# Row sums of a softmax: partial sums on GpSimd, ones-products once per pair of heads, and another step order

## The chip, the cores and the metric

The kernel runs on one core of a Trainium2 chip. The metric is the device time of one execution in microseconds (us); for a kernel that was timed in several runs it is their median. Engines are named as in the profile: PE (TensorE), ACT (ScalarE), DVE (VectorE), POOL (GpSimd), SP (the engine that issues most DMAs).

## What is computed

A two-layer backbone over 512 latent tokens of width 1024, in float32. Layer 0 mixes tokens by an 8-head latent attention and a Fourier mixer; layer 1 by a convolution module and a short gated convolution; each layer ends with a SwiGLU. All modulations come from a matrix-vector product with the conditioning vector (below: the ada jobs). The change lies in the attention of layer 0, which for each head is

```python
kt = jnp.concatenate([k_ctx, k], axis=1)      # 256 context + 512 latent keys
s = jnp.einsum('bqhd,bhkd->bhqk', q, kt) * scale
p = jax.nn.softmax(s, axis=-1)
o = jnp.einsum('bhqk,bhkd->bqhd', p, vt)
...
mix = o @ a_w_out                              # after concatenation with the Fourier part
```

with 512 queries, 768 keys, 96 elements of q and k and 64 of v per head.

## The kernel before, in words

Matmul operands are split into a high and a low part (`split`, L94: ACT casts the high part at L95, DVE, or in layer 1 partly GpSimd, subtracts at L96), and `mm3` (L115 to L117) takes three products. Weights arrive as units of 128x1024 floats (`unit`, L102): SP issues the load (L105) into one of three buffers of the tag `wraw`, and the halves go to `whi` and `wlo`, five buffers each.

Attention goes head by head, with keys in the partitions: the score tile is transposed, so that exp(score - maximum) can be taken by ACT straight out of PSUM. For head h the steps are

- `m0`, `m1` (`a_max`): the maxima of the **next** head. PE computes rough scores (L821, L822), DVE reduces them from PSUM (L824, L825); `m1` ends with the maximum of two small SBUF tiles (L827) and its negation into `nmx` (L828).
- `row` (`a_row`): PE transposes `nmx` (L836) and ACT copies the row to row 96 of the next head's `qT` (L837), so that a score matmul subtracts the maximum itself. The next head's first score (L850) needs it.
- `s0`, `s1`, `s2` (`a_score`): each two tiles of 128 keys by 512 queries, three matmuls each (L850 to L852) and an exponential on ACT (L853) into a 128x1024 tile: a buffer of `wraw` (named `praw`) or a fixed slot.
- `tq`, `tk`, `tc` (`a_trq`, `a_trk`): transposes of q and k of the head after the next, taken out of PSUM by ACT (L787) and DVE (L788).
- After two heads (a pair): `v0` to `v2`, or `p0` to `p2` when they come among the next pair's steps (`a_av`): the products with v (L865), and behind them four products with a matrix of ones (L870), which sum the exponentials over the keys. In the last of them ACT copies the sums (L874) and the output (L876) to SBUF.
- `n0` to `n2` (`a_nrm`): the sums are picked out by a small matmul with `sel` (L884) and inverted by DVE (L886); PE spreads the inverse over 64 rows (L892); DVE multiplies (L898), and the result is split into `o_t`, which out_proj reads.

`EVEN_ORDER` and `ODD_ORDER` give the order in which a head's steps are written, and `weave` puts the ada jobs between them, each of which is one load and one DVE operation of 128x1024 with two SBUF inputs (L153). The last pair's products and normalization stand in `END_ORDER`, between the first steps "O" of out_proj: L525 to L552, `unit` m, then the products of output block m. A scheduler then moves the instructions on each engine by its own estimates, so the written order is not the order of an engine. Each engine takes its own instructions strictly in order. PSUM has eight buffers (`ps`, L82).

Of the kernel before, what the change touches and what calls it, by code (L numbers as in the profile page):

```python
# [9 lines left out]
F32 = mybir.dt.float32  # L10
# [7 lines left out]
P = 128  # L18
D = 1024
KT = 8  # L20
S = 512
# [3 lines left out]
NH = 8  # L25
# [8 lines left out]
FH = (5, 14)  # L34
PH = (2, 3)
HU, NF, NK2 = (14, 13, 8), 5, 5
EVEN_ORDER = "m0 p1 p2 s0 m1 s1 s2 n0 tk row n1 n2 tq tc"
ODD_ORDER = "s0 s1 m0 s2 m1 v0 row tk tc tq"
END_ORDER = "p1 p2 O n0 O n1 n2 O O O"
OA = 4  # L40
MIX_ORDER = "G0 G3 G2 C0 G1 C2 C3 C1"
SA0, SA1, SC, PU, RB, TB, AB = 1, 20, 15, 6, 3, 5, 2
# [3 lines left out]
UB = 5  # L46
# [14 lines left out]
def tile_dit(  # L61
# [16 lines left out]
    def nm(base):  # L78
        uid[0] += 1
        return f"{base}_{uid[0]}"  # L80

    def ps(shape=(P, S)):  # L82
        return pp.tile([P, S], F32, tag="ps", name=nm("ps"))

    def t2k(n=S):
        return tmp.tile([P, n], F32, tag="t", bufs=TB, name=nm("t"))
# [753 lines left out]
    def a_score(h, tp):  # L840
        def f():
            kT, qT = kTt[h % 2], ost["qT"][:, h % 2]
            raw = ost["pb"][(3 * h + tp) % 6]
            if raw is None:
                raw = units.tile([P, D], F32, tag="wraw", bufs=RB, name=nm("praw"))
            for s in range(2):
                t = tp * 2 + s
                c = slice(t * P, (t + 1) * P)
                p = ps()
                T.matmul(p, kT[:97, 0, c], qT[:97, 0, :], start=True, stop=False)  # L850
                T.matmul(p, kT[:96, 0, c], qT[:96, 1, :], start=False, stop=False)  # L851
                T.matmul(p, kT[:96, 1, c], qT[:96, 0, :], start=False, stop=True)  # L852
                A.activation(raw[:, s * S:(s + 1) * S], p, AF.Exp, scale=float(DH) ** -0.5)  # L853
            ost["p", h, tp] = raw
        return f

    def a_av(j, tp):
        def f():
            if tp == 0:
                ost["o", j], ost["su", j] = ps(), ps()  # L860
            p, su = ost["o", j], ost["su", j]
            for s in range(2):
                t = tp * 2 + s
                for x in range(2):
                    T.matmul(p[64 * x:64 * x + 64, :], vh[t][:, 2 * j + x, :], ost["p", 2 * j + x, tp][:, s * S:(s + 1) * S],  # L865
                             start=(t == 0), stop=(t == 5))
            for s in range(2):
                for x in range(2):
                    g = 32 * (2 * x + s)
                    T.matmul(su[g:g + 32, :], ones[:, 0:32], ost["p", 2 * j + x, tp][:, s * S:(s + 1) * S],  # L870
                             start=(tp == 0), stop=(tp == 2), tile_position=(0, g))
            if tp == 2:
                ost["sr", j] = t2k()
                A.copy(ost["sr", j], su)  # L874
                ost["or"] = t2k()
                A.copy(ost["or"], p)  # L876
        return f

    def a_nrm(j, i):
        def f():  # L880
            if i == 0:
                st = ps()
                for t in range(4):
                    T.matmul(st[:, 2 * t:2 * t + 2], ost["sr", j][:, t * P:(t + 1) * P], sel, start=True, stop=True)  # L884
                r = sm.tile([P, 8], F32, tag="rs", name=nm("rs"))
                V.reciprocal(r, st[:, 0:8])  # L886
                ost["r"] = r
            elif i == 1:
                ost["rb"] = ps()
                for t in range(4):  # L890
                    for x in range(2):
                        T.matmul(ost["rb"][64 * x:64 * x + 64, t * P:(t + 1) * P],  # L892
                                 ost["r"][:, 2 * t + x:2 * t + x + 1].to_broadcast([P, 64]), ident, start=True, stop=True)
            else:
                if j % 2 == 0:
                    o_t.append(slot((9, 10)[j // 2], [P, 2, 2, S], F32R))
                d = o_t[j // 2][:, j % 2]
                V.tensor_mul(ost["or"], ost["or"], ost["rb"])  # L898
                split(d[:, 0, :], d[:, 1, :], ost["or"])
        return f  # L900
# [7 lines left out]
    for h in range(NH):  # L908
        made = {f"s{i}": a_score(h, i) for i in range(3)}
        if h + 1 < NH:  # L910
            made.update(m0=a_max(h + 1, 0), m1=a_max(h + 1, 1), row=a_row(h + 1))
        if h + 2 < NH:
            made.update(tq=a_trq(h + 2), tk=a_trk(h + 2, 2, 4), tc=a_trk(h + 2, 0, 2))
        j = h // 2
        made.update({f"v{i}": a_av(j, i) for i in range(3)})
        if j > 0:
            made.update({f"p{i}": a_av(j - 1, i) for i in range(3)})
            made.update({f"n{i}": a_nrm(j - 1, i) for i in range(3)})
        asteps += [made[x] for x in (EVEN_ORDER, ODD_ORDER)[h % 2].split() if x in made]
    g1s = ada_jobs(0, "g1", 16, 8)  # L920
    s2s = ada_jobs(0, "s2", 24, 16)
# [20 lines left out]

    oout = out_proj(w_out0, 8, mix(0), mix(1), mods[0, "g1"], "n2_0", n2_0)
    end = {f"p{i}": a_av(NH // 2 - 1, i) for i in range(3)}
    end.update({f"n{i}": a_nrm(NH // 2 - 1, i) for i in range(3)})
    last, pos = [], 0
    for x in END_ORDER.split():
        if x == "O":
# [485 lines left out]
```

## Time and profile before

| | |
|---|---|
| median of 3 runs | 1205.73 us (1203.50 to 1205.98) |
| the profiled execution | 1207.13 us, its span 1205.4 us |
| granted TensorE clock of the span | 0.995 of full speed |
| attention, first score to first product of the last pair | 147.76 to 239.59 us of the span |
| out_proj's second unit begins | 254.93 us |

The profile shows one execution. Times in it are microseconds from the start of the span; matmul records overlap, since they are pipelined, so the distance from start to start tells what one costs. Products with 64 or 32 output columns of weights in float32 leave two records per matmul.

### The profile page before, as it was taken

The page shows a single profiled execution, that of the slowest core. Times are in us where ns is not written, and L with a number is a line of the kernel's source. Part 1 is how long each engine was busy: PE and PEld are TensorE (multiplying, and loading weights), DVE is VectorE, ACT ScalarE, POOL GpSimd, SP SyncE. Part 2 cuts the span into 40 slices and gives each one's busy share as a digit, 9 for nine tenths or more (in the row PEclk, how much of TensorE's full clock was granted, in tenths as well). Part 3 has the DMA queues.
Part 4 walks back from the last instruction along what each step waited for, and adds up shares of the span by engine and source line. Part 5 has one row for each costly group of instructions (what it writes and reads, how often), then busy time and mean ns, then how long its engine had stood idle before and what let it go on. Part 6 is the DMA issues. An engine that isn't in the chain of part 4 may idle for free.

```text
span 1205.4 us, 16811 instructions
## 1 busy us (share of the span) xinstructions
PE 1180.0 (98%) x6627; PEld 994.7 (83%) x6627; DVE 800.9 (66%) x1302; ACT 480.0 (40%) x787; POOL 128.0 (11%) x110
## 2 busy tenths in 40 slices
PE   8999999999999999999999899999899999999998
PEld 6777856569988888888888888889898899989987
DVE  7989877647655556554443799967867458746861
ACT  5545455535332323232222554335644235424530
POOL 1013300000000000000004495100000000000000
PEclk9999999999999999999999999999999999999999
DMA  9872033383265565555555232221357336634341
GB/s 345 299 290 86 1 110 101 112 271 124 86 210 191 195 207 184 186 182 166 166 166 154 74 105 89 86 88 36 134 149 207 115 98 171 188 96 128 92 140 53
DMA packets 52226, 177.25 MB, mean 147 GB/s; under 512 B 5681, under 2 KB 6577, under 8 KB 51890
## 3 DMA queue, kind: packets, MB, share of 16 engines
q1 hardware_dynamic: 49410, 166.21, 41.5%
q0 software_dynamic: 2736, 9.96, 4.9%
q8 instruction: 52, 0.85, 0.3%
q14 instruction: 28, 0.23, 0.1%
HBM read 174.05 MB, written 2.10 MB: 146 GB/s over the span
## 4 chain that ended last, share of the span: by engine, by line
PE 90%; DVE 4%; DMA 3%; ACT 2%; issue 1%; SPq 0%; POOL 0%; ACTq 0%; DVEq 0%
PE ps L115 21%; PE ps L117 21%; PE ps L116 21%; PE ps L1135 14%; PE ps L865 2%; DMA wraw<-in_w 1%; PE ps L707 1%; DVE wlo L96 1%; PE ps L580 1%; PE ps L850 1%; PE ps L851 1%; PE ps L852 1%; ACT whi L95 1%; PE ps L870 1%; DVE t L210 1%
## 5 line engine op out<-in xcount | busy, mean ns | idle before, releaser
L115 PE MATMUL ps<-s,whi 128*128 128x512 f32 (+1 forms) x1067 | 395.8, 371 | 7.0 <-ACT whi L95 5.8
L116 PE MATMUL ps<-s,whi 128*128 128x512 f32 (+1 forms) x1067 | 391.7, 367 | 2.1 <-DVE s L216 2.1
L117 PE MATMUL ps<-s,wlo 128*128 128x512 f32 (+1 forms) x1067 | 391.7, 367 | 1.4 <-DVE wlo L96 1.4
L95 ACT CAST whi<-wraw 128x1024 fp32r<-128x1024 f32 (+1 forms) x133 | 135.7, 1022 | 319.0 <-PE ps L116 184.4
L115 PEld LDWEIGHTS ps<-s,whi 128*128 128x128 f32 x1067 | 202.1, 190 | 42.4 <-ACT whi L95 7.1
L117 PEld LDWEIGHTS ps<-s,wlo 128*128 128x128 f32 x1067 | 202.0, 189 | 36.9 <-DVE wlo L96 3.2
L116 PEld LDWEIGHTS ps<-s,whi 128*128 128x128 f32 x1067 | 202.2, 190 | 35.7 <-DVE s L216 2.3
L96 DVE TENSOR_TENSOR wlo<-wraw,whi 128x1024 fp32r<-128x1024 f32 (+2 forms) x113 | 134.0, 1186 | 89.9 <-ACT whi L95 86.0
L1135 PE MATMUL ps<-s,whi 128*128 128x256 f32 x912 | 168.1, 285 | 2.1 <-DVE t L1155 2.1
L1135 PEld LDWEIGHTS ps<-s,whi 128*128 128x128 f32 x912 | 143.1, 192 | 4.5 <-DVE t L1155 3.5
L1135 PE MATMUL ps<-s,wlo 128*128 128x256 f32 x456 | 128.5, 283 | 0.0
L271 DVE SCALAR_TENSOR_TENSOR x<-ps,m_g,x 128x512 f32<-128x512 f32 (+1 forms) x67 | 43.9, 661 | 104.9 <-PE ps L117 104.9
L153 DVE CUSTOM_DVE_ANT_0 ada<-ada,scb,vec 128x1024 f32<-128x1024 f32 x80 | 100.1, 1278 | 1.1 <-DMA ada<-in_ada 1.1
L1135 PEld LDWEIGHTS ps<-s,wlo 128*128 128x128 f32 x456 | 87.4, 192 | 0.0
L1102 POOL DMA_DIRECT2D s<-in_w x19 | 16.8, 884 | 606.3 <-DMA s<-in_w 414.6
L96 DVE TENSOR_TENSOR wlo<-s,whi 128x1024 fp32r<-128x1024 f32 x57 | 69.4, 1221 | 11.7 <-ACT whi L95 11.3
L95 ACT CAST whi<-s 128x1024 fp32r<-128x1024 f32 x57 | 58.8, 1044 | 28.0 <-PE ps L116 19.1
L1007 DVE TENSOR_TENSOR t<-ps,t 128x512 f32<-128x512 f32 x22 | 15.2, 692 | 71.3 <-PE ps L117 71.3
L1247 DVE SCALAR_TENSOR_TENSOR ps<-s,vec,ps 128x512 f32<-128x512 f32 x78 | 55.8, 748 | 1.4 <-ACT ps L1244 0.9
L96 POOL TENSOR_TENSOR wlo<-wraw,whi 128x1024 fp32r<-128x1024 f32 x20 | 49.2, 2462 | 30.9 <-ACT whi L95 27.0
L116 PE MATMUL ps<-s,s 128*128 128x256 f32 (+1 forms) x160 | 50.2, 315 | 0.0
L117 PE MATMUL ps<-s,s 128*128 128x256 f32 (+1 forms) x160 | 50.1, 314 | 0.0
(274 smaller groups left out, 1608.2 us busy)
## 6 DMA issues: line engine op xcount, KB each, us to landing
ada<-in_ada SPq DMA_DIRECT2D x82, 512.0 KB, 4.4
wraw<-in_w SPq DMA_DIRECT2D x74, 512.0 KB, 3.7
s<-in_w SPq DMA_DIRECT2D x19, 768.0 KB, 5.1
wraw<-in_w_in SPq DMA_DIRECT2D x20, 512.0 KB, 3.3
s<-in_w SPq DMA_DIRECT2D x38, 256.0 KB, 4.3
s<-in_w POOLq DMA_DIRECT2D x19, 512.0 KB, 5.5
s<-in_ada SPq DMA_DIRECT2D x16, 512.0 KB, 6.7
wraw<-in_w_out SPq DMA_DIRECT2D x16, 512.0 KB, 3.8
```

Of the source, the lines that this page charges most:

```text
L95: A.copy(hi, src)
L96: (eng or V).tensor_sub(lo, src, f32(hi))
L115: T.matmul(o, wh, ah, start=start, stop=False)
L116: T.matmul(o, wh, al, start=False, stop=False)
L117: T.matmul(o, wl, ah, start=False, stop=stop)
L153: i = V.tensor_tensor_reduce(raw, raw, scv, 1.0, vc("ada_b", idx), ALU.mult, ALU.add, accum_out=dst)
L271: V.scalar_tensor_tensor(X[m][:, a:b], psum, gcol, X[m][:, a:b], ALU.mult, ALU.add)
L865: T.matmul(p[64 * x:64 * x + 64, :], vh[t][:, 2 * j + x, :], ost["p", 2 * j + x, tp][:, s * S:(s + 1) * S], start=(t == 0), stop=(t == 5))
L1007: V.tensor_mul(g, p, held.pop(f))
L1102: G.dma_start(s13, w[:, :D], accum_op=ALU.add)
L1135: T.matmul(o, w, b, start=start and kk == 0 and i == 0, stop=kk == 3 and i == 2, skip_group_check=True)
L1247: V.scalar_tensor_tensor(dst, cp[:, w:w + S], vec[:, o + w:o + w + 1], src, ALU.mult, ALU.add)
```

## The change

Per head, GpSimd adds the three tiles of exponentials elementwise into one tile `psum` of 128x1024, a buffer of the tag `wlo`: one addition after the exponentials of `s1`, one after those of `s2`. The ones-products read `psum` and are made once per pair, as a step of their own: it is the new `n0`, which also copies the sums, and the old `n0` to `n2` become `n1` to `n3`. The three orders are rewritten for it; in them `m0`, `m1` and `row` stand at other places too.

```diff
--- before.py
+++ after.py
@@ -34,9 +34,9 @@
 FH = (5, 14)
 PH = (2, 3)
 HU, NF, NK2 = (14, 13, 8), 5, 5
-EVEN_ORDER = "m0 p1 p2 s0 m1 s1 s2 n0 tk row n1 n2 tq tc"
-ODD_ORDER = "s0 s1 m0 s2 m1 v0 row tk tc tq"
-END_ORDER = "p1 p2 O n0 O n1 n2 O O O"
+EVEN_ORDER = "m0 p1 p2 n0 s0 m1 s1 n1 s2 tk n2 row n3 tq tc"
+ODD_ORDER = "s0 m0 s1 m1 s2 v0 tk row tc tq"
+END_ORDER = "p1 p2 O n0 n1 O n2 n3 O O O"
 OA = 4
 MIX_ORDER = "G0 G3 G2 C0 G1 C2 C3 C1"
 SA0, SA1, SC, PU, RB, TB, AB = 1, 20, 15, 6, 3, 5, 2
@@ -852,26 +852,24 @@
                 T.matmul(p, kT[:96, 1, c], qT[:96, 0, :], start=False, stop=True)
                 A.activation(raw[:, s * S:(s + 1) * S], p, AF.Exp, scale=float(DH) ** -0.5)
             ost["p", h, tp] = raw
+            if tp == 1:
+                ost["sum", h] = units.tile([P, D], F32, tag="wlo", bufs=UB, name=nm("psum"))
+                G.tensor_add(ost["sum", h], ost["p", h, 0], raw)
+            elif tp == 2:
+                G.tensor_add(ost["sum", h], ost["sum", h], raw)
         return f
 
     def a_av(j, tp):
         def f():
             if tp == 0:
-                ost["o", j], ost["su", j] = ps(), ps()
-            p, su = ost["o", j], ost["su", j]
+                ost["o", j] = ps()
+            p = ost["o", j]
             for s in range(2):
                 t = tp * 2 + s
                 for x in range(2):
                     T.matmul(p[64 * x:64 * x + 64, :], vh[t][:, 2 * j + x, :], ost["p", 2 * j + x, tp][:, s * S:(s + 1) * S],
                              start=(t == 0), stop=(t == 5))
-            for s in range(2):
-                for x in range(2):
-                    g = 32 * (2 * x + s)
-                    T.matmul(su[g:g + 32, :], ones[:, 0:32], ost["p", 2 * j + x, tp][:, s * S:(s + 1) * S],
-                             start=(tp == 0), stop=(tp == 2), tile_position=(0, g))
             if tp == 2:
-                ost["sr", j] = t2k()
-                A.copy(ost["sr", j], su)
                 ost["or"] = t2k()
                 A.copy(ost["or"], p)
         return f
@@ -879,13 +877,23 @@
     def a_nrm(j, i):
         def f():
             if i == 0:
+                su = ps()
+                for s in range(2):
+                    for x in range(2):
+                        g = 32 * (2 * x + s)
+                        T.matmul(su[g:g + 32, :], ones[:, 0:32], ost["sum", 2 * j + x][:, s * S:(s + 1) * S],
+                                 start=True, stop=True, tile_position=(0, g))
+                sr = t2k()
+                A.copy(sr, su)
+                ost["sr", j] = sr
+            elif i == 1:
                 st = ps()
                 for t in range(4):
                     T.matmul(st[:, 2 * t:2 * t + 2], ost["sr", j][:, t * P:(t + 1) * P], sel, start=True, stop=True)
                 r = sm.tile([P, 8], F32, tag="rs", name=nm("rs"))
                 V.reciprocal(r, st[:, 0:8])
                 ost["r"] = r
-            elif i == 1:
+            elif i == 2:
                 ost["rb"] = ps()
                 for t in range(4):
                     for x in range(2):
@@ -915,7 +923,7 @@
         made.update({f"v{i}": a_av(j, i) for i in range(3)})
         if j > 0:
             made.update({f"p{i}": a_av(j - 1, i) for i in range(3)})
-            made.update({f"n{i}": a_nrm(j - 1, i) for i in range(3)})
+            made.update({f"n{i}": a_nrm(j - 1, i) for i in range(4)})
         asteps += [made[x] for x in (EVEN_ORDER, ODD_ORDER)[h % 2].split() if x in made]
     g1s = ada_jobs(0, "g1", 16, 8)
     s2s = ada_jobs(0, "s2", 24, 16)
@@ -942,7 +950,7 @@
 
     oout = out_proj(w_out0, 8, mix(0), mix(1), mods[0, "g1"], "n2_0", n2_0)
     end = {f"p{i}": a_av(NH // 2 - 1, i) for i in range(3)}
-    end.update({f"n{i}": a_nrm(NH // 2 - 1, i) for i in range(3)})
+    end.update({f"n{i}": a_nrm(NH // 2 - 1, i) for i in range(4)})
     last, pos = [], 0
     for x in END_ORDER.split():
         if x == "O":
```

Line numbers behind the additions shift: the products with v are L870 in the changed kernel, the ones-products L884, the copies of outputs and of sums L874 and L887, the product with `sel` L892, the reciprocal L894, the spreading L900, the multiplication L906. The additions are L857 and L859.

How the instructions stand on POOL in the attention of layer 0, where there were none before (`praw`, `s_245` and `s6b` hold exponentials, heads 0 and 1 shown; 16 in all, two per head):

```order
L857 TENSOR_TENSOR psum_1454<-praw_1421,s_245_1297 128x1024
L859 TENSOR_TENSOR psum_1454<-psum_1454,praw_1456 128x1024
L857 TENSOR_TENSOR psum_1531<-s_245_1297,praw_1520 128x1024
L859 TENSOR_TENSOR psum_1531<-psum_1531,s6b_1298 128x1024
```

All sixteen read two tiles in SBUF.

DVE in head 2, where the maxima of head 3 are finished (`mx`; `s_242` is `nmx`, `rs` the inverse sums, `ada` an ada job). Before:

```order
L825 TENSOR_REDUCE mx_1591<-ps_1636 128x2
L827 TENSOR_TENSOR mx_1591<-mx_1591 128x4
L828 TENSOR_SCALAR s_242_1291<-mx_1591 128x4
L153 ISA ada_1669,m_g_935<-ada_1669,scb,vec 128x1024
L153 ISA m_g_935 128x1
L886 RECIPROCAL rs_1677<-ps_1672 128x8
```

Now:

```order
L825 TENSOR_REDUCE mx_1592<-ps_1634 128x2
L894 RECIPROCAL rs_1663<-ps_1658 128x8
L827 TENSOR_TENSOR mx_1592<-mx_1592 128x4
L153 ISA ada_1665,m_g_935<-ada_1665,scb,vec 128x1024
L153 ISA m_g_935 128x1
L828 TENSOR_SCALAR s_242_1291<-mx_1592 128x4
```

The reciprocal has come ahead of the maxima, and an ada job stands between the two small operations that finish them. The heads 3 and 6 have the ada job at the same place.

ACT at the end of attention (`t` is a copy of sums or outputs, `whi` a unit's high part). Before:

```order
L95 CAST whi_2222<-wraw_2221 128x1024
L874 COPY t_2217<-ps_2189 128x512
L876 COPY t_2219<-ps_2188 128x512
L95 CAST whi_2261<-wraw_2260 128x1024
L159 ACTIVATE m_s_936<-m_s_936,vec 128x1
L95 CAST whi_2304<-wraw_2303 128x1024
L95 CAST whi_2336<-wraw_2335 128x1024
```

Now:

```order
L95 CAST whi_2207<-wraw_2206 128x1024
L874 COPY t_2204<-ps_2188 128x512
L95 CAST whi_2253<-wraw_2252 128x1024
L159 ACTIVATE m_s_936<-m_s_936,vec 128x1
L95 CAST whi_2296<-wraw_2295 128x1024
L95 CAST whi_2328<-wraw_2327 128x1024
L887 COPY t_2243<-ps_2238 128x512
```

The copy of the sums has moved from behind the first unit's cast to behind the fourth's. On PE, the last ones-products and the product with `sel` stand now between units 0 and 1:

```order
L117 MATMUL ps_2212<-s_442_2146,wlo_2208 128x512
L884 MATMUL ps_2238<-psum_2175,ones 32x512
L884 MATMUL ps_2238<-psum_2107,ones 32x512
L884 MATMUL ps_2238<-psum_2175,ones 32x512
L892 MATMUL ps_2245<-sel,t_2243 128x2 x4
L115 MATMUL ps_2258<-s_93_707,whi_2253 128x512
```

Before, the product with `sel` stood there alone; the first of the four ones-products of this step has gone further forward, behind unit 0's first products.

## Rows read from the trace of the kernel before

**Rows 1.** The page, part 1: busy time of each engine.

```profile
PE 1180.0 (98%) x6627; PEld 994.7 (83%) x6627; DVE 800.9 (66%) x1302; ACT 480.0 (40%) x787; POOL 128.0 (11%) x110
```

**Rows 2.** Windows: stretch, length, busy time (instructions) per engine, granted clock, DMA share, GB/s.

```profile
147.76:239.59 91.83, 91.39 (x503) 55.90 (x501) 66.52 (x122) 47.77 (x88) 0.00 (x0) 1.00 0.34 103
```

**Rows 3.** Chain of waits, 160 to 171 us: start, length, engine, tile, line.

```profile
160.54 1.87 PE ps L865 x8
162.41 1.00 PE ps L870 x8
163.41 1.00 PE ps L865 x2
...
166.00 1.86 PE ps L865 x6
167.86 0.98 PE ps L870 x2
...
169.72 0.99 PE ps L870 x6
```

**Rows 4.** Timeline, layers 0 and 1: start, length, engine, line, operation, out<-in.

```profile
601.83 0.69 DVE L280 TENSOR_TENSOR acc<-acc,t 128x512 f32<-128x512 f32 x1
...
644.85 1.05 ACT L95 CAST whi<-wraw 128x1024 fp32r<-128x1024 f32 x1 [3.10 <-PE ps L116]
...
645.98 2.40 POOL L96 TENSOR_TENSOR wlo<-wraw,whi 128x1024 fp32r<-128x1024 f32 x1 [1.26 <-ACT whi L95]
...
646.49 2.44 DVE L280 TENSOR_TENSOR acc<-acc,t 128x512 f32<-128x512 f32 x1 [0.70 <-ACT t L279]
```

**Rows 5.** Timeline, GpSimd and VectorE around 714 us (mixer of layer 1).

```profile
714.04 5.22 POOL L96 TENSOR_TENSOR wlo<-wraw,whi 128x1024 fp32r<-128x1024 f32 x2
...
715.83 1.17 DVE L1319 SCALAR_TENSOR_TENSOR t<-s,vec,t 128x512 f32<-128x512 f32 x1 [0.21 <-ACT t L1318]
...
717.58 2.23 DVE L1320 SCALAR_TENSOR_TENSOR t<-s,vec,t 128x512 f32<-128x512 f32 x1
```

**Rows 6.** Timeline of head 0, from the exponentials to the next head's first score.

```profile
150.75 1.30 ACT L853 ACTIVATE s<-ps 128x512 f32<-128x512 f32 x2 [0.81 <-PE ps L852]
...
152.16 1.29 ACT L853 ACTIVATE praw<-ps 128x512 f32<-128x512 f32 x2
...
152.51 0.16 DVE L827 TENSOR_TENSOR mx<-mx 128x4 f32<-128x4 f32 x1
...
152.78 1.28 DVE L153 CUSTOM_DVE_ANT_0 ada<-ada,scb,vec 128x1024 f32<-128x1024 f32 x1
...
153.00 0.56 PE L836 MATMUL ps<-identr,s 128*97 128x128 f32 x4
...
154.04 0.58 ACT L837 CAST s<-ps 1x512 fp32r<-1x512 f32 x1
...
154.67 0.50 PE L850 MATMUL ps<-s,s 97*128 97x512 f32 x1 [0.44 <-ACT s L837]
```

**Rows 7.** Timeline of the end of attention and the start of out_proj.

```profile
239.59 0.64 PE L865 MATMUL ps<-praw,s 128*64 128x512 f32 x1
...
242.60 6.02 SPq L105 DMA_DIRECT2D wraw<-in_w_out  x3
...
247.31 1.04 ACT L95 CAST whi<-wraw 128x1024 fp32r<-128x1024 f32 x1 [6.90 <-DMA wraw<-in_w_out]
...
248.39 1.23 DVE L96 TENSOR_TENSOR wlo<-wraw,whi 128x1024 fp32r<-128x1024 f32 x1 [7.95 <-ACT whi L95]
...
251.28 0.37 SPq L105 DMA_DIRECT2D wraw<-in_w_out  x1
...
254.12 0.95 PE L884 MATMUL ps<-sel,t 128*128 128x2 f32 x8
...
254.93 0.48 PE L115 MATMUL ps<-s,whi 128*128 128x512 f32 x1
...
257.59 1.05 ACT L95 CAST whi<-wraw 128x1024 fp32r<-128x1024 f32 x1 [3.93 <-DMA wraw<-in_w_out]
```

## The prediction, made before the changed kernel ran

> **What bounds the kernel now.** I read four views. The page's busy times come first [rows 1]: PE is busy 98% of the span and POOL 11%, so a saving on PE counts only if it lies on the path, and POOL has time to spare. Then the windows of the stretch that the change touches, from the first score to the last pair's first product with v [rows 2]: 91.39 of 91.83 us are PE, at full clock, and POOL does nothing there. PE sets this stretch, and a PE instruction removed from it is worth its whole spacing unless something else comes late. Then the chain, for prices on PE [rows 3], and the timeline, for what happens where GpSimd and DVE work side by side [rows 4, 5] and for the short path of the maxima [rows 6]. The end of the stretch is another regime: PE waits for weights there [rows 7], so I cost it by itself.
>
> **PE, attention.** A step of products with v costs 1.87 us for its eight records, and a step of ones-products 1.00 [rows 3]. The products run in pairs side by side; where other work cuts a step at an odd place, 2 and 6 records cost 1.00 + 1.86 = 2.86 instead of 1.87, and 2 and 6 ones-records 0.98 + 0.99 instead of 1.00. So a cut costs about 1.0. Before, three of four pairs have their three ones-steps inside the stretch: 9 x 1.0, and one cut, 10.0 removed. The order of the change has the products with v cut three times where it was five: 2.0 removed. Added are three ones-steps, one per pair, 1.0 each and 0.08 for the change of tile shape: 3.2. Net -12.0 + 3.2 = **-8.8**.
>
> **GpSimd's additions.** The trace has this operation on the same shape: a subtraction of two 128x1024 SBUF tiles takes 2.40 us and starts 0.08 after ACT has made its input (644.85 + 1.05, then 645.98) [rows 4]. Two per head are 4.8 us in a head of some 11, off the path by themselves, since the ones-products come a pair later. But see what such an operation does to DVE: the addition L280, also with two SBUF inputs, takes 0.69 alone and 2.44 beside GpSimd, ending 0.55 after GpSimd's does (648.93 and 648.38), so that it ran only once GpSimd was through [rows 4]. Another such pair: two GpSimd operations from 714.04 to 719.26, a DVE operation of two SBUF inputs at 717.58 that takes 2.23 and one at 715.83 that takes 1.17, coming in between the two [rows 5]. So a DVE instruction that reads two SBUF tiles stands still until the GpSimd instruction under way ends, and the next instruction of either goes to whoever waited longer. The Trainium skill ("SBUF — State Buffer", section "Who interferes with whom") speaks against the change in the same way: a VectorE instruction with two SBUF inputs contends with a GpSimd instruction that reads SBUF, and the pair of ports they share is held for a whole instruction; by it the additions are not free, as 2.44 against 0.69 agrees.
>
> Which DVE instructions of a head have two SBUF inputs? The maximum L827 (0.16 us) and the ada jobs L153 (1.28) [rows 6], and L96 of the normalized output. The reductions and L788 read PSUM. L827 is on the way to the next head's score: in head 0, L827 starts at 152.51, the transposition L836 at 153.00, the copy L837 at 154.04, and the score at 154.67 [rows 6]. Walking the order of the change with these durations, I get for PE's wait at each head's end, against a row of instructions without waits:
>
> - Head 0: the exponentials of s1 end at 152.05; an addition would run from 152.13 to 154.53. L827 slips by 2.0, L836 comes at 154.95, the copy ends about 155.9 and the score at 156.0 instead of 154.67 [rows 6]. That is 1.3 more than before, where PE had waited 0.5 here: 1.8.
> - Head 1: the ada job behind head 0's maxima waits for the second addition, the L788 behind it frees its PSUM buffer late (1.0), and L827 meets the second addition (1.4, and 0.2 of passing on): 2.6.
> - Head 2: L827 waits for the first addition's end; the second is then due and takes the port; the ada job between L827 and L828 waits for it, 2.4, and takes 1.28; L828, then L836, is 3.5 late.
> - Heads 3 and 4: `row` stands behind products with v, or L828 ahead of the ada job: 0.4 and 0.
> - Head 5: two ada jobs and L96 stand ahead of the maxima, each behind an addition: 4.0.
> - Head 6: as head 2 but with no transposes ahead of L836, 4.0; and on ACT the cast of the output, which waits for DVE's multiplication, stands ahead of L837, 1.0: 5.0.
>
> Sum 17.3. Before, the stretch had 2.0 of waits and short fillings beyond its row of instructions (89.8 of the 91.83 when I add up start-to-start distances); they are replaced. So the stretch changes by -8.8 + 17.3 - 2.0 = **+6.5**. The bounds of this term: without any blocking PE keeps head 0's 0.5 and about half of the rest (0.75), and gets ACT's delay at head 6: the multiplication, 0.69 if it goes by L280 [rows 4], the cast of half a tile's 0.6 and the copy's 0.58 [rows 6], 1.85 together: -8.8 - 0.75 + 1.85 = -7.7. If L828, with one SBUF input, is blocked too, each of two heads pays 2.2 more: +10.9. I take the middle one, because rows 4 and 5 show the blocking on this very operation.
>
> **The end of attention.** Before, unit 0's load goes out at 242.60, when the first products have released its buffer, and lands at 247.31, 4.71 later; unit 1 starts at 254.93, that is 15.34 after the first product of the last pair at 239.59 [rows 7]. Now the ones-products behind that first step are gone: the load goes out 1.0 sooner, the cast begins at +6.7 and ends at +7.8 and the low part at +9.0 (1.04 and 1.23) [rows 7]. PE has only 5.6 of products with v and waits, so the shorter PE work buys nothing but this 1.0. What is late next is the copy of the sums: ACT has it behind the casts of units 1, 2 and 3. The fourth unit's load needs the first `wraw` buffer, free at +9.0; issue at about +9.35, landing 4.7 later, cast 1.05, copy 0.6, 0.15 to pass on, and the product with `sel` 0.8 until unit 1 may start (254.12 to 254.93) [rows 7]: +16.65 against +15.34, **+1.3**. With a landing of 6.3, as that fourth load took before (251.28 to 257.59) [rows 7], +2.9. Below: if the scheduler's place of the copy hurt nothing, unit 1 would start 1.0 sooner, -1.0. I take +1.3. Behind it nothing changes: out_proj and all that follows issue the same instructions.
>
> **Sum.** +6.5 + 1.3 = +7.8 on a profiled execution of 1207.13: 1214.9. The median of the runs lies 1.4 lower, at 1205.73; on it, **1213.5**. The likeliest case's own range is 1208 to 1219.
>
> **Rivals.**
> 1. *The blocking does not matter here* (faster). Then the stretch gives -7.7, the end +1.3: -6.4, 1199.3. For it: PE's saving is real in rows 2 and 3, and a DVE instruction of 0.16 us may slip in before the addition starts, when the exponentials end a little later than I walk. Against it: L827 comes 0.5 after the exponentials of s1 in head 0, in the midst of the addition. Chance 0.29.
> 2. *DVE wins the port* between two additions at heads 2 and 6. The ada job then goes ahead of the second addition and L828 is 2.4 sooner, twice: -4.8, so +3.0, 1208.7. For it: the DVE instruction at 715.83 did get in between two of GpSimd's [rows 5]. Against: in both heads the second addition is due before L827 has ended. With some slack more it ends within the noise. Chance 0.12.
> 3. *L828 is blocked as well* (slower still): 4.4 more, 1218. For it speaks no row: L828 follows L827 at once wherever it stands. Chance 0.07.
> The forecast has 0.52. That the additions are not made by GpSimd at all is excluded by the order of the program: sixteen stand on POOL.
>
> **How the numbers follow.** A measurement of this kernel can tell about 0.2% (2.4 us) from no change. Faster by more: rival 1, 0.29. Within: rival 2, 0.12. Slower: forecast and rival 3, 0.59. The range leaves out less than 2 in 10: from 1198, just under rival 1, to 1219, the forecast with the slow landing and part of rival 3.
>
> **What would show it.** In the changed profile: sixteen POOL operations of about 2.4 us between 150 and 245; L153 and L827 at more than their 1.28 and 0.16, up to 3.7 and 2.5, where these run; PE idle before L850 released by ACT's L837, 1 to 5 us at heads 0, 1, 2, 5 and 6 and none at 3 and 4; the first product of the last pair near 246; unit 1 of out_proj some 16.7 after it, released by the copy L887. Wrong if L827 keeps 0.16 everywhere or the stretch is shorter than 91.8: then the blocking is no price here. If DVE is blocked and the stretch is still shorter, PE had other work ready, and I have walked the order too strictly.

## The result, and the profile after

The changed kernel takes 1220.59 us (median of 6 runs, 1216.75 to 1224.30) against 1205.85 before: a ratio of 1.0119, 95% interval 1.0098 to 1.0140, so 14.7 us slower, where 7.8 were forecast. The direction holds; the size is nearly twice the forecast and lies outside its range.

The page of the changed kernel, part 1, answers to [rows 1]:

```profile
span 1222.5 us, 16711 instructions
...
PE 1181.5 (97%) x6563; PEld 999.4 (82%) x6563; DVE 818.2 (67%) x1302; ACT 481.6 (39%) x787; POOL 169.4 (14%) x126
```

Its profiled run took 1224.30 us, the longest of the six. The windows row of the same stretch as in [rows 2], first score to the last pair's first product with v:

```profile
147.39:252.22 104.83, 91.44 (x455) 59.08 (x453) 84.12 (x123) 49.86 (x88) 36.53 (x15) 0.92 0.32 101
```

The stretch has become 104.83 us where it was 91.83: +13.0 against the +6.5 of the forecast. Two things are to be read in the row. PE is busy 91.44, so 13.4 are waits; and although 24 products with ones are gone (two records each, 455 records for 503), the busy time has not fallen, and the granted clock is 0.92 where it was 1.00. These are two losses, and only the first was forecast.

**The waits.** PE's timeline, all its waits over 0.3 us in the stretch but one, which stands in the next fence (the bracket: idle before, and who ended it):

```profile
154.39 0.56 PE L836 MATMUL ps<-identr,s 128*97 128x128 f32 x4 [1.52 <-DVE s L828]
...
158.38 0.50 PE L850 MATMUL ps<-s,s 97*128 97x512 f32 x1 [0.37 <-DVE s L788]
...
165.95 0.53 PE L836 MATMUL ps<-identr,s 128*97 128x128 f32 x4 [1.31 <-DVE s L828]
...
217.51 0.50 PE L821 MATMUL ps<-s,s 96*128 96x512 f32 x1 [2.79 <-ACT s L787]
...
244.12 0.92 PE L836 MATMUL ps<-identr,s 128*97 128x128 f32 x4 [3.34 <-DVE s L828]
245.97 0.80 PE L850 MATMUL ps<-s,s 97*128 97x512 f32 x1 [0.93 <-ACT s L837]
```

Head 0 waits 1.52, head 1 0.37 and 1.31, head 2 2.99, head 5 2.79, head 6 3.34 and 0.93; heads 3 and 4 nothing. The sum is 13.3 of the 13.4. How one comes about is seen in head 2, on the timeline of POOL, DVE and PE:

```profile
178.10 2.38 POOL L857 TENSOR_TENSOR psum<-praw,s 128x1024 f32<-128x1024 f32 x1 [12.53 <-ACT s L853]
...
178.28 2.22 DVE L827 TENSOR_TENSOR mx<-mx 128x4 f32<-128x4 f32 x1
...
180.43 1.27 DVE L153 CUSTOM_DVE_ANT_0 ada<-ada,scb,vec 128x1024 f32<-128x1024 f32 x1
180.56 3.33 POOL L859 TENSOR_TENSOR psum<-psum,praw 128x1024 f32<-128x1024 f32 x1
...
181.63 2.29 DVE L828 TENSOR_SCALAR s<-mx 128x4 fp32r<-128x4 f32 x1
...
184.07 0.53 PE L836 MATMUL ps<-identr,s 128*97 128x128 f32 x4 [2.99 <-DVE s L828]
```

L827 needs 0.16 us [rows 6] and takes 2.22, until the addition beside it ends. Then the ada job, which the new order has put ahead of L828, gets the port, and the second addition, due at 180.56, takes 3.33 because it waits for the job. L828 comes last and waits for that addition, 2.29 us for an instruction of 0.17. PE, free since 181.08, starts L836 at 184.07.

Head 5 comes about by another way, on the timeline of DVE and ACT before the wait of 2.79:

```profile
211.41 3.40 DVE L153 CUSTOM_DVE_ANT_0 ada<-ada,scb,vec 128x1024 f32<-128x1024 f32 x1
...
215.41 1.27 DVE L153 CUSTOM_DVE_ANT_0 ada<-ada,scb,vec 128x1024 f32<-128x1024 f32 x1
...
216.72 0.39 ACT L159 ACTIVATE m_s<-m_s,vec 128x1 f32<-128x1 f32 x1 [3.01 <-DVE m_s L153]
```

An ada job waits for an addition and makes the next one late; ACT waits 3.01 us for the result of the second, which it has to scale (L159), and L787, for which PE waits, stands behind that on ACT.

**The clock.** Windows of 2 us around the end of that wait (length; busy time of PE, PEld, DVE, ACT and POOL; granted clock; DMA):

```profile
182.00:184.00 2.00, 0.00 (x0) 0.00 (x0) 2.00 (x2) 0.00 (x0) 1.90 (x1) 1.00 0.65 156
184.00:186.00 2.00, 1.93 (x12) 1.61 (x13) 1.27 (x3) 1.31 (x3) 0.00 (x0) 0.81 0.30 115
186.00:188.00 2.00, 2.00 (x7) 1.52 (x6) 2.00 (x4) 1.53 (x3) 0.00 (x0) 0.50 0.00 0
...
190.00:192.00 2.00, 2.00 (x6) 1.52 (x6) 1.83 (x4) 0.60 (x1) 0.00 (x0) 0.50 0.34 139
192.00:194.00 2.00, 2.00 (x11) 1.50 (x9) 1.63 (x3) 1.01 (x2) 1.25 (x1) 0.99 0.51 119
```

PE waited with the clock at 1.00; about 1.2 us after it resumed the clock fell to 0.50, which is 1.2 GHz, and stayed there until about 192, with PE busy throughout. The same comes with the waits of heads 5 and 6, in head 6 already within the wait. In windows of 1 us, busy time times the missing share of the clock gives 3.4, 1.7 and 2.5 us, 7.6 together.

**The end of attention**, rows that answer to [rows 7]:

```profile
252.22 0.64 PE L870 MATMUL ps<-praw,s 128*64 128x512 f32 x1
...
254.21 6.05 SPq L105 DMA_DIRECT2D wraw<-in_w_out  x4
...
257.54 1.04 ACT L95 CAST whi<-wraw 128x1024 fp32r<-128x1024 f32 x1 [4.56 <-DMA wraw<-in_w_out]
...
265.95 0.59 ACT L887 COPY t<-ps 128x512 f32<-128x512 f32 x1 [0.42 <-PE ps L884]
...
266.59 1.05 PE L892 MATMUL ps<-sel,t 128*128 128x2 f32 x8 [0.72 <-ACT t L887]
267.50 0.48 PE L115 MATMUL ps<-s,whi 128*128 128x512 f32 x1
```

Unit 1 starts 15.28 us after the last pair's first product, against 15.34: +1.3 was forecast, -0.1 came. The load went out 2.0 after that product as worked out, but the copy of the sums started at +13.7 where the forecast's steps give +15.1: the first load had landed 3.3 us after its issue (257.54), where 4.7 was taken, so its buffer, and with it the fourth load, came sooner.

Up to unit 1 of out_proj the profiled run has lost 12.6 us (267.50 against 254.93). The remaining 4.5 of the difference of the spans lie in layer 1. A chain row of the kernel before, and two of the changed one, at the same load of weights:

```profile
925.84 5.27 DMA wraw<-in_w
```

```profile
937.73 6.88 DMA wraw<-in_w
...
947.84 0.43 PE ps L115
```

That load took 1.6 us longer, and the products behind it ran at 0.43 instead of 0.23, at the lower clock, until 953. In the profiled runs of the kernel before and of the kernels below (without e11_noada, which moves work there) the time behind unit 1 is 947.8 to 953.4 us; that the 955.0 here belongs to the change rather than to this run was not shown. The clock fell behind that load in the profiled runs of e2 and e13 below too, for about half as long. The interval of the ratio, 11.8 to 16.9 us, holds the 12.6.

### The profile page after: what moved, and what is told of

Its sections match the earlier page's. It is cut to its first block, busy times and chain, and to the rows that moved or that the text cites. A ratio compares the mean times of both kernels' runs of the same rounds, so it can differ in the third digit from the quotient of the medians.

```text
span 1222.5 us, 16711 instructions
## 1 busy us (share of the span) xinstructions
PE 1181.5 (97%) x6563; PEld 999.4 (82%) x6563; DVE 818.2 (67%) x1302; ACT 481.6 (39%) x787; POOL 169.4 (14%) x126
## 4 chain that ended last, share of the span: by engine, by line
PE 87%; DVE 6%; DMA 3%; ACT 2%; issue 1%; SPq 0%; POOL 0%; ACTq 0%; DVEq 0%
PE ps L115 22%; PE ps L117 21%; PE ps L116 21%; PE ps L1143 13%; PE ps L870 2%; DMA wraw<-in_w 1%; PE ps L707 1%; PE ps L580 1%; DVE wlo L96 1%; DVE ada L153 1%; ACT whi L95 1%; DVE mx L827 1%; DMA s<-in_w 1%; DVE t L210 1%; PE ps L850 1%
## 5 line engine op out<-in xcount | busy, mean ns | idle before, releaser
L153 DVE CUSTOM_DVE_ANT_0 ada<-ada,scb,vec 128x1024 f32<-128x1024 f32 x80 | 104.4, 1331 | 0.0
```

The costliest lines, as they stand in the source:

```text
L153: i = V.tensor_tensor_reduce(raw, raw, scv, 1.0, vc("ada_b", idx), ALU.mult, ALU.add, accum_out=dst)
```

## The experiments

"Stretch" is always first score to the last pair's first product with v; "unit 1" is the start of out_proj's second unit counted from that product, and unit 0 in the text that of its first. Ratios are to the kernel before, run on the same chip in turn.

| run | stretch | unit 1 | ratio (95% interval) |
|---|---|---|---|
| before | 91.83 | 15.34 | 1 |
| the change | 104.83 | 15.28 | 1.0119 (1.0098 to 1.0140) |
| e1_noadd | 87.57 | 15.37 | 0.9965 (0.9953 to 0.9978) |
| e2_reduce | 91.33 | 15.40 | 0.9994 (0.9976 to 1.0013) |
| e3_oldorder | 86.70 | 20.13 | 0.9993 (0.9977 to 1.0009) |
| e4_neworder | 91.91 | 14.31 | 0.9993 (0.9976 to 1.0009) |
| e5_nonegate | 95.10 | 15.31 | 1.0034 (1.0016 to 1.0053) |
| e6_oldreduce | 82.83 | 19.46 | 0.9957 (0.9943 to 0.9971) |
| e7_halves | 94.87 | 15.19 | 1.0030 (1.0015 to 1.0044) |
| e8_fill | 105.42 | 15.49 | 1.0108 (1.0090 to 1.0126) |
| e9_sa19 | 83.76 | 20.54 | 0.9973 (0.9960 to 0.9986) |
| e10_sa18 | 83.24 | 19.59 | 0.9967 (0.9956 to 0.9979) |
| e11_noada | 87.25 | – | not timed |
| e12_beforereduce | 91.81 | 15.50 | 1.0006 (0.9991 to 1.0022) |
| e13_lastdve | 82.83 | 15.65 | 0.9927 (0.9915 to 0.9939) |

### Additions or order: e1, e3, e4

e1_noadd, the change without the additions:

```diff
-            if tp == 1:
-                ost["sum", h] = units.tile([P, D], F32, tag="wlo", bufs=UB, name=nm("psum"))
-                G.tensor_add(ost["sum", h], ost["p", h, 0], raw)
-            elif tp == 2:
-                G.tensor_add(ost["sum", h], ost["sum", h], raw)
...
-  T.matmul(su[g:g + 32, :], ones[:, 0:32], ost["sum", 2 * j + x][:, s * S:(s + 1) * S],
+  T.matmul(su[g:g + 32, :], ones[:, 0:32], scb[:, s * S:(s + 1) * S],
```

> Leaves out: GpSimd's sixteen additions; the ones-products, once per pair as in the change, read a constant 128x1024 tile instead of the sums, so the normalization is not that of the reference. Order and number of PE's instructions as in the change. Theory (GpSimd's additions hold back the DVE instructions that finish the maxima, and PE's clock falls in the waits): L827 back at 0.16 us, no wait of PE before L836 over 0.5, clock 0.99; first score to first product of the last pair about 84 us (91.8 before, 104.8 in the changed kernel); 1199 (1196 to 1202). Rival (the new places of the maxima and their transposition make them late, whoever adds): the waits before L836 stay, 1214 to 1220.

17 us of stretch are gone with the additions. PE, ACT and DVE each have the same instructions in the same order in this stretch as in the change, so the additions are the cause. The stretch is 87.6 and not 84, and the total of 1202.85 is just above the expected range. The reason is a wait that needs no addition (timeline of PE, and the windows row of the stretch):

```profile
229.03 0.50 PE L850 MATMUL ps<-s,s 97*128 97x512 f32 x1 [1.62 <-ACT s L837]
```

```profile
147.39:234.96 87.57, 85.32 (x454) 55.09 (x452) 66.55 (x123) 49.59 (x88) 0.00 (x0) 0.98 0.39 120
```

At head 6, L837 stands behind the cast of the output on ACT, which I had walked; the clock then falls behind this wait of 1.62 as well, which costs 1.7 us by windows of 1 us, and PE's busy time is 85.3 where 82 is to be had with the old places (e6 below).

e3_oldorder, the change with the maxima and their transposition at their old places:

```diff
-EVEN_ORDER = "m0 p1 p2 n0 s0 m1 s1 n1 s2 tk n2 row n3 tq tc"
-ODD_ORDER = "s0 m0 s1 m1 s2 v0 tk row tc tq"
+EVEN_ORDER = "m0 p1 p2 n0 s0 m1 s1 s2 n1 tk row n2 n3 tq tc"
+ODD_ORDER = "s0 s1 m0 s2 m1 v0 row tk tc tq"
```

> The change with the additions on GpSimd and the ones-products once per pair, but m0, m1 and row at their places of before in both orders. Theory: even heads have the maxima at the same place behind s1 and meet the additions as in the change, odd heads meet the second addition; slower than before, 1208 to 1220. Rival of the order: the PE work saved shows, 1197 to 1201.

Neither: no slower than before, but no faster. The stretch is 86.7: L827 still takes up to 2.00 us beside an addition, but L828 follows it at once, no wait of PE is over 1.53, and the clock is 1.00 throughout. The 5 us gained are lost again behind it, at out_proj (20.1 instead of 15.3), to which e6 comes back.

e4_neworder, the kernel before with the new places and no additions:

```diff
-EVEN_ORDER = "m0 p1 p2 s0 m1 s1 s2 n0 tk row n1 n2 tq tc"
-ODD_ORDER = "s0 s1 m0 s2 m1 v0 row tk tc tq"
+EVEN_ORDER = "m0 p1 p2 s0 m1 s1 n0 s2 tk n1 row n2 tq tc"
+ODD_ORDER = "s0 m0 s1 m1 s2 v0 tk row tc tq"
```

> The kernel before with m0, m1, row and the normalization at the places of the change, no additions, ones-products in every step as before. Theory: no wait to speak of, PE does what it did: 1203 to 1208. Rival of the order: 1212 or more.

The time, 1205.56 us, is as the theory says, although the wait of 1.62 in head 6 is there as well; the clock stays up behind it. So the new order without additions costs nothing in the kernel before, the additions and the saved products together come out even with the old order, and with the new order they cost 14.7 us. Where the products with ones are saved, the new order does cost something without any addition: e1's stretch is 4.7 us longer than that of e6 below, which has the old one.

### Which instructions wait: e2, e5, e7, e11, e12

e2_reduce, the change with the maxima finished by one reduction of a strided view, and with a transposition by minus the identity:

```diff
-                V.tensor_max(mx[:, 0:4], mx[:, 0:4], mx[:, 4:8])
-                V.tensor_scalar(ost["nmx"][:, :, 96], mx[:, 0:4], -1.0, None, ALU.mult)
+                V.reduce_max(ost["nmx"][:, :, 96], mx.rearrange("p (a t) -> p t a", a=2), axis=AX.X)
...
-    A.copy(identr, ident)
+    A.mul(identr, ident, -1.0)
```

> The additions stay on GpSimd. The maximum of two SBUF tiles (L827) and the negation (L828) become one reduction over a strided view of one tile that writes nmx, and the sign goes into the matrix of the transposition. Theory: the reduction takes its 0.2 us beside a running addition, the path of the maxima is free; the ada jobs still wait up to 2.4 and free a PSUM buffer late at one or two heads, 1 to 2 us: stretch 84 to 87, 1199 to 1204. Second rival (every DVE instruction that reads SBUF waits, one source or two): the reduction takes up to 2.4 as well, 1212 to 1220. Rival of the order: 1214 to 1220.

The timeline of its head 2:

```profile
175.06 2.39 POOL L856 TENSOR_TENSOR psum<-praw,s 128x1024 f32<-128x1024 f32 x1 [11.08 <-ACT s L852]
...
175.24 0.11 DVE L827 TENSOR_REDUCE s<-mx 128x4 fp32r<-128x8 f32 x1
...
175.27 3.26 DVE L153 CUSTOM_DVE_ANT_0 ada<-ada,scb,vec 128x1024 f32<-128x1024 f32 x1
```

The reduction, which reads SBUF too, takes 0.11 us in the midst of an addition; over all eight heads it takes 0.11 to 0.17. The ada job behind it waits, 3.26 instead of 1.28. 13.5 us of stretch are back. The expectation was 84 to 87 and 91.3 came: waits of 0.68, 1.80 and 2.35 are left, the last with the lower clock behind it.

e11_noada takes the ada jobs away as well, all of them moved behind attention:

```diff
-SA0, SA1, SC, PU, RB, TB, AB = 1, 20, 15, 6, 3, 5, 2
+SA0, SA1, SC, PU, RB, TB, AB = 1, 1, 15, 6, 3, 5, 2
```

> The change with the reduction in place of maximum and negation, and no ada job among attention's steps (all come behind them, so the end of the kernel's first half gets longer and the total says nothing; only the stretch is read). Theory (what was left of waits in the run with the reduction, 0.7, 1.8 and 2.4 us, comes from ada jobs waiting for additions and holding up DVE): the first two go, the last falls to the 1.6 of ACT's order, stretch 83 to 86 instead of 91.3. Rival (the additions delay something else too): stretch 88 or more.

The waits of 0.68 and 1.80 are gone and that of head 6 is 1.62, all as the theory says; the stretch, 87.25, lies just between the two expectations, because behind that 1.62 the clock falls as in e1 (PE is busy 85.05), which the expectation had left out. Blocked ada jobs, for whose results ACT waits with L787 behind (head 5 above), are the second part of the loss.

e5_nonegate keeps the maximum of two SBUF tiles and drops L828:

```diff
-                V.tensor_max(mx[:, 0:4], mx[:, 0:4], mx[:, 4:8])
-                V.tensor_scalar(ost["nmx"][:, :, 96], mx[:, 0:4], -1.0, None, ALU.mult)
+                V.tensor_max(ost["nmx"][:, :, 96], mx[:, 0:4], mx[:, 4:8])
...
-    A.copy(identr, ident)
+    A.mul(identr, ident, -1.0)
```

> The change, but the maximum (still of two SBUF tiles) writes nmx itself and the sign goes into the matrix of the transposition, so that the negation L828 is gone. Theory (L828, with one SBUF input, waited 2.29 us for the addition at heads 2 and 6, and each of these two waits of PE was followed by some 6 us at the lower clock): the waits of 2.99 and 3.34 us before the transposition go to under 1.2 and the clock stays up behind them; the wait of 2.79 at head 5 stays with its low clock; stretch 91 to 95 us (104.8 in the change), 1206 to 1211. Rival (L827 and the ada job between them cost the time, L828 only passes it on): stretch 100 or more, 1216 to 1220.

9.7 us of stretch go with L828 alone: 95.10 is at the upper end of the expectation, and the total of 1210.43 us is within it. The wait of 2.99 at head 2 is gone, with its low clock. PE's timeline shows where the clock still falls:

```profile
210.85 0.50 PE L821 MATMUL ps<-s,s 96*128 96x512 f32 x1 [1.94 <-ACT s L787]
...
237.08 0.50 PE L849 MATMUL ps<-s,s 97*128 97x512 f32 x1 [2.49 <-ACT s L836]
```

These are head 5, by the ada jobs, and head 6, mostly by ACT's order (1.62 in e1, without additions).

e7_halves cuts each addition in two:

```diff
-                G.tensor_add(ost["sum", h], ost["p", h, 0], raw)
+                for c in (slice(0, S), slice(S, D)):
+                    G.tensor_add(ost["sum", h][:, c], ost["p", h, 0][:, c], raw[:, c])
...
-                G.tensor_add(ost["sum", h], ost["sum", h], raw)
+                for c in (slice(0, S), slice(S, D)):
+                    G.tensor_add(ost["sum", h][:, c], ost["sum", h][:, c], raw[:, c])
```

> The change, each addition cut into two of 512 columns (1.2 to 1.3 us each). Theory: an instruction of DVE waits for the one under way only, so at most 1.3; waits before the transposition at heads 2 and 6 fall to 0.5 to 1.5, and the clock stays up at least behind one of them; stretch 88 to 97, 1204 to 1213. Rival (GpSimd keeps the port over back-to-back instructions): as the change, 1217 to 1222.

As expected: 94.87, and 1208.86 us in total. The timeline of POOL and DVE in its head 2:

```profile
175.63 2.51 POOL L858 TENSOR_TENSOR psum<-praw,s 128x512 f32<-128x512 f32 x2 [11.81 <-ACT s L853]
178.34 3.24 POOL L861 TENSOR_TENSOR psum<-psum,praw 128x512 f32<-128x512 f32 x2 [0.20 <-POOL psum L858]
...
176.52 0.40 DVE L827 TENSOR_TENSOR mx<-mx 128x4 f32<-128x4 f32 x1
176.85 2.38 DVE L153 CUSTOM_DVE_ANT_0 ada<-ada,scb,vec 128x1024 f32<-128x1024 f32 x1
...
179.16 1.22 DVE L828 TENSOR_SCALAR s<-mx 128x4 fp32r<-128x4 f32 x1
```

L827 waits 0.24, the ada job 1.1 and L828 1.05, each between two pieces of additions, which are 1.27 long. GpSimd does not keep the port over back-to-back instructions.

e12_beforereduce, the control, is the kernel before with e2's edit.

> The kernel before with the reduction in place of maximum and negation and nothing else: a control. Theory: no port is shared there, no wait goes: 1204 to 1207. Rival (the reduction alone brought the gain of the version with the old places): 1199 to 1202.

No difference: the reduction gains nothing where GpSimd does nothing beside it.

### What the clock costs: e8

```diff
             p = ps()
+            if h in (3, 7):
+                for _ in range(11):
+                    T.matmul(p, kTt[(h - 1) % 2][:96, 0, 0:P], ost["qT"][:96, (h - 1) % 2, 0, :], start=True, stop=True)
             for t in range(4):
```

> The change with eleven added products of 512 columns (0.235 us each, results not used) ahead of the transposition in heads 2 and 6, where PE waits 2.99 and 3.34 us. They add work on PE and take no wait away from DVE. Theory (some 3 us behind each of these waits are lost to the lower clock alone): the clock stays up behind both, the stretch is 98 to 100 instead of 104.8, 1213 to 1216. Rival (the lower clock costs nothing, because ACT or DVE are the bound there): 1219 to 1222.

The stretch misses the expectation with 105.4, and the total of 1219.11 us lies where the rival has it. But at head 2 the experiment does what it should (timeline of PE, then two windows behind it, columns as above):

```profile
181.59 2.82 PE L837 MATMUL ps<-s,s 96*128 96x512 f32 x11
184.61 0.56 PE L839 MATMUL ps<-identr,s 128*97 128x128 f32 x4 [0.20 <-DVE s L828]
...
187.10 0.50 PE L853 MATMUL ps<-s,s 97*128 97x512 f32 x1 [1.27 <-ACT s L840]
```

```profile
188.00:190.00 2.00, 2.00 (x11) 1.67 (x10) 2.00 (x6) 1.31 (x3) 0.00 (x0) 1.00 0.19 43
190.00:192.00 2.00, 2.00 (x11) 1.67 (x10) 2.00 (x4) 1.20 (x2) 0.41 (x1) 1.00 0.54 219
```

The fills take PE's wait, and the clock stays at 1.00 in the windows where the change had 0.50. From L836 to the next product with v it is 8.29 us (184.61 to 192.90) where the change needs 10.05 (184.07 to 194.12), and these 8.29 hold a wait of 1.27 that the change did not have, since the scheduler also moved L837 behind other work of ACT. Without it the lower clock's price there is 3.0 us, near the 3.4 of the windows; between these marks PE has the same 36 records in the same order in both. At head 6 the same move of L837 makes a wait of 3.64, the clock falls all the same, and the gain is eaten. So the price of the lower clock is shown at head 2 alone; at heads 5 and 6 it rests on the windows.

### A version faster than both: e6, e9, e10, e13

e6_oldreduce is e3's order with e2's reduction.

> The additions and the ones-products once per pair, the places of before for the maxima and their transposition, and the reduction in place of maximum and negation. Theory: the four waits of 0.4 to 1.5 us before the transposition in the run with the old places go, stretch 83 to 85 (86.7 there, 91.8 before); unit 1 of out_proj starts 15.3 to 20 after it, by whether the last ada job still meets an addition and holds up SP; 1198 to 1203. Rival (something else than the port makes the maxima late there): no gain over the run with the old places, 1204 to 1207.

1200.18 us against 1205.73. The windows row of its stretch:

```profile
146.74:229.57 82.83, 81.96 (x455) 54.88 (x453) 69.86 (x115) 48.43 (x88) 40.89 (x15) 1.00 0.36 115
```

This is what the change had to give: PE 81.96 busy where it was 91.39 [rows 2], almost no wait, full clock. But unit 1 starts 4.1 later than before (timeline of DVE, POOL, SP and PE at the end of attention):

```profile
229.23 3.38 DVE L153 CUSTOM_DVE_ANT_0 ada<-ada,scb,vec 128x1024 f32<-128x1024 f32 x1
...
228.95 2.58 POOL L856 TENSOR_TENSOR psum<-s,praw 128x1024 f32<-128x1024 f32 x1 [1.39 <-ACT praw L852]
...
233.08 7.17 SPq L105 DMA_DIRECT2D wraw<-in_w_out  x4
...
238.63 0.68 PE L115 MATMUL ps<-s,whi 128*128 128x512 f32 x1 [3.69 <-ACT whi L95]
```

An ada job meets the last head's additions and takes 3.38 (to 232.61); SP, which needs its buffer for the next ada load (issued at 232.65), stands still with out_proj's first load behind it, and PE waits 3.69. e9_sa19 and e10_sa18 move one and two ada jobs (`SA1` 19 and 18) behind attention.

> The version with the old places and the reduction, with one ada job fewer among attention's steps and one more behind them. There the last ada job waited for an addition (3.38 us instead of 1.28), SP waited for it with the next ada load, and out_proj's first load, behind that in SP's queue, went out at 3.5 us after the last pair's first product instead of 2.0. Theory: with that job away the load goes out 1.0 to 1.5 sooner, PE's wait falls from 3.7 to some 2.3, the clock stays up, unit 1 starts 15.3 to 17 us after that product instead of 19.5; 1196 to 1199. Rival (another ada load takes its place in the queue): 1199 to 1202.

> As the run before it, with two ada jobs fewer among attention's steps; one ada load now stands between out_proj's second and third load. Theory: first load as early, third load some 0.5 to 1.5 later, hidden by PE's work on the units before it: 1196 to 1200. Rival as there: 1199 to 1202.

Both miss, with 1202.56 and 1201.82 us: unit 0 stays at 9.1 to 9.2, because another ada job stands at the same place and takes 3.38 us in each. e13_lastdve takes the last head's additions off GpSimd instead:

```diff
-                G.tensor_add(ost["sum", h], ost["p", h, 0], raw)
+                (V if h == NH - 1 else G).tensor_add(ost["sum", h], ost["p", h, 0], raw)
...
-                G.tensor_add(ost["sum", h], ost["sum", h], raw)
+                (V if h == NH - 1 else G).tensor_add(ost["sum", h], ost["sum", h], raw)
```

> The version with the old places and the reduction, and the two additions of the last head on DVE instead of GpSimd. In the runs with 18, 19 and 20 ada jobs alike the ada job that stands behind the last head's maxima took 3.38 us beside GpSimd's last additions, and out_proj's first load waited for the ada load that waits for it. Theory (that chain of ada job, SP and load makes the end late): without an addition of GpSimd beside it the job takes 1.28, the load goes out 2.0 us after the last pair's first product instead of 3.5, unit 0 starts 6.4 to 7.5 after it instead of 9.1, unit 1 15.3 to 17 instead of 19.5; 1196 to 1199. Rival (the load itself is late with the old places, for its buffer or its transfer): unit 0 stays at 9, 1199 to 1203.

```profile
230.10 1.22 DVE L856 TENSOR_TENSOR psum<-s,praw 128x1024 f32<-128x1024 f32 x1
...
232.56 1.28 DVE L153 CUSTOM_DVE_ANT_0 ada<-ada,scb,vec 128x1024 f32<-128x1024 f32 x1
...
232.43 0.33 SPq L105 DMA_DIRECT2D wraw<-in_w_out  x1
233.88 0.33 SPq L152 DMA_DIRECT2D ada<-in_ada  x1
...
237.21 0.50 PE L115 MATMUL ps<-s,whi 128*128 128x512 f32 x1 [1.41 <-ACT whi L95]
```

On this timeline of DVE, SP and PE the job takes 1.28, the load goes out 2.0 after the first product (230.44), unit 0 starts at +6.8 and unit 1 at +15.65, and the kernel takes 1198.47 against 1206.94, 0.7% less than before. So the loss at out_proj goes with the last head's two additions on GpSimd. But SP's order is another here: the load goes out before the ada job has even begun, and the ada load behind which it stood in e6 follows it. In e6 the trace shows SP waiting for the blocked job; that the shorter job alone, with SP's order of e6, would bring the same was not shown.

## Why the prediction was right in direction and wrong in size

- *PE's saving*, -8.8: right for the instructions that it counts. By start-to-start distances less waits, the products with ones and with v cost 31.7 us in the stretch before and 22.6 in the change, -9.2. (The 0.08 for the change of tile shape stands in no row; the three added steps came to 2.99 us.) What the sum leaves out is that the other instructions rise with the new order at full clock, by some 1.6: the transposes of q and k cost 6.7 before, 8.2 in the change, and without any addition 7.7 in e1 and 7.5 in e4.
- *The blocking*: right. L827 takes up to 2.22, ada jobs up to 3.40, and without the additions (e1) or with a reduction in place of L827 and L828 (e2) the stretch is 17 and 13.5 us shorter.
- *The waits*, 17.3 by the walk: 13.3 measured, head by head 1.52, 1.68, 2.99, 0, 0, 2.79 and 4.27 where the walk had 1.8, 2.6, 3.5, 0.4, 0, 4.0 and 5.0. The walk had the second addition go before the ada job and L828 free of blocking; in fact the job went first, as rival 2 said, and L828 was blocked, as rival 3 said, and the two nearly cancel: that 3.5 came near 2.99 in head 2 is luck. The waits stand before L836, and in head 5 before L821, and not before L850 as I had it, but for 0.37 in head 1 and 0.93 in head 6. The Trainium skill ("SBUF — State Buffer", "Who interferes with whom") lists tensor_scalar among the operations that can, under conditions on their operands, take both ports, and says that tensor_reduce never contends on this chip; L828 with 2.29 and e2's reduction with 0.11 agree with both. I had L828's case as a rival with too small a chance.
- *The step that failed* is the sum -8.8 + 17.3 - 2.0 = +6.5: it counts PE's instructions at their full-clock spacing behind each wait, and so puts the lower clock at nothing. I had set out waits as long as these and asked of none what PE's clock does behind it. PE's busy time was 91.4, and 7.6 us of it are the price of three stretches at 1.2 GHz behind the waits of 2.79 to 3.34 us (3.0 at head 2 by e8, where the windows give 3.4; the rest by the windows alone). Without them 83.8 is left; e6 has 82.0 with the old order, and e1, e2 and e11, with the new one, have 83.3 to 84.1 when their own low clock is taken off in the same way, so the difference of some 1.8 goes with the order.
- *How the parts add up*: -9.2 for the products, +1.6 for the other instructions, +7.6 for the clock and +13.0 for waits (13.4 where before had 0.4) make the +13.0 of the stretch. The forecast had +15.3 for waits, 17.3 less 2.0. That its waits were 2.4 too long hid part of the missing clock; with the waits as they came the same sum would have said about +4.
- *The end*, +1.3: -0.1; the first load landed after 3.3 us, where I took 4.7 from before.
- *The median*: 12.6 us are shown by the landmarks; the other 2.1 of the 14.7 lie within the interval, and where they come from stays open.

## What to carry to other kernels

An engine with time to spare is not free if it shares a port: before work goes to GpSimd, list the VectorE instructions with SBUF inputs on the path beside it, and finish short critical steps by reductions or out of PSUM (in e2 the product of a PSUM and an SBUF tile took 0.67 us in the midst of an addition, as long as it takes alone). Price a wait of TensorE with what the lower clock behind it may cost as well; here 7.6 us beside 13.3 of waits. And look for who waits for a blocked job in turn: an ada job held up SP, and SP the weights of the next stage.

## What the runs showed that I had not expected

- L828, a negation of 128x4 with one SBUF input, took 2.29 us beside a GpSimd addition where it needs 0.17; a reduction from SBUF did not wait at all (0.11 to 0.17).
- Between GpSimd instructions back to back the port goes to a waiting DVE instruction: waits of 0.24 to 1.1 us beside pieces of 1.27 (e7).
- The clock fell behind waits of PE of 1.36 (e7), 1.62 (e1, e11) and 1.94 us (e5), and not behind 1.62 in e4 and 1.80 in e2. What else decides was not settled.
